# The last two products of a decoder block by seven products for all eight units, and norms summed by two wide matmuls

## The chip, the core and the metric

The kernel runs on one core of a Trainium2 chip. A core has TensorE (PE, matrix products into PSUM), VectorE (DVE), ScalarE (ACT), GpSimd (POOL) and SyncE (SP), which here only issues DMAs; ACT's queue issues the stores. The metric is the time of one execution in microseconds of device time, here the median of three runs.

## The reference

A block over x of 1024 x 2048 in fp32: a norm, one input projection into five parts of width 1024, two branches (a gated MLP and a gated recurrence), a norm of each, an output projection, a norm with residual, and a gated embedding:

```python
hn = rmsnorm(h, pre_g[l])
z = hn @ w_in[l]
u, v, gate_a, xb, gate_b = jnp.split(z, splits, axis=-1)
ya = gmlp_branch(u, v, ...) * jax.nn.silu(gate_a)
yb = rglru_branch(xb, ...) * jax.nn.silu(gate_b)
y = jnp.concatenate([rmsnorm(ya, gmlp_out_g[l]), rmsnorm(yb, lru_out_g[l])], axis=-1)
h = h + rmsnorm(y @ w_out[l], post_g[l])
h = h + (p[l] @ w_pe[l]) * jax.nn.sigmoid(h @ w_pg[l])
```

The change is about the products with `w_out` ("o", weights `w_o1`, `w_o2`) and `w_pg` ("z" or "h", weights `w_g1`, `w_g2`), both 1024 x 2048 by 2048 x 2048, and about the three norms after the first.

## The kernel before, in words

**Precision.** Each fp32 operand is cut in a head and a rest, both of a type that PE takes at one pass (`split`: ACT copies the head, DVE subtracts it from the source, L133 and L124). A product is three: head by head, rest by head, head by rest.

**Quarters and units.** An activation is kept transposed as four quarters q = 2 i + j, where i is the half of the 2048 features and j the half of the 1024 positions; a quarter has four blocks c of 128 x 2 x 512. A unit u is a pair of 128 output columns, one in each half. A unit by the four quarters is a 2x2 product of blocks, eight block products if it is done plainly, seven by the Strassen-Winograd scheme with sums of activations (T1 to T4) and of weights (s1 to s4).

**Steps.** One block product over 1024 features is 24 matmuls of 128x512, and that is a `Step`; a group of n units takes its steps n at a time. `issue` goes through the steps in order: it issues the weight loads three steps ahead, prepares the weights (sums, head and rest) two steps ahead, the activations up to three steps ahead (`lead`), moves spawned tasks on by one (`tick`; a task yields how many steps it waits), and emits the products. `early` holds calls that are to come before a given step; `ahead` fills it. A load by `load_late` waits for the first product of the step before. The framework places the instructions on the engines' queues, which run in order. Buffers: five raw weight tiles, three prepared ones, 32 tiles for activations, four for loads, eight of 512 columns, eight PSUM banks.

**Acts** makes an activation operand when it is first asked for: `fetch` loads the block (scaled by norm and gain the first time, and stored), sums are subtracted on DVE, and `put` splits. For T4, T2 is loaded again from memory.

**The two last products.** In either, units 0 and 1 are plain (`Group.plain`, eight steps with the quarters 21 and 11, and later eight with 22 and 12). Units 2 to 7 go through `set1` (products with 11, 21, T2, T1: 24 steps, with results for two quarters put away) and then `Last2` (with T3, T4, 22: 18 steps). In the last product `OutZ` adds, beside these steps, the products with `w_e` (192 matmuls, L1161), then sigmoid, product and sum with h, and the store.

**Norms.** `norm` sums squares of columns over partitions by narrow products (`rms_small`, L158: a 128x128 block of squares against a column of ones, in fp32), takes the root on 128x4, and spreads the result over partitions with diagonal matrices (`spread`, L173 and L178). `fetch_y` and `fetch_h` then scale with a column of gains and the norm, both on DVE (L1018, L1090).

Of the kernel before, what the change touches and what calls it, by code (L numbers as in the profile page):

```python
# [13 lines left out]
P = 128  # L14
# [3 lines left out]
NH = 8  # L18
# [22 lines left out]
B1 = (2, 2, 2, 1, 1)  # L41
# [7 lines left out]
def block_kernel(ctx: ExitStack, tc: tile.TileContext, xq, pT, w_v, w_l1, w_l2, w_u1, w_u2, w_o1, w_o2, w_g1,  # L49
                 w_g2, w_e, wsT, w_ax, cols, bs, outq):  # L50

# [140 lines left out]
    def norm(accs, n, s, j, wait):  # L192

        yield wait
        small = cpool.tile([P, 4], F32, tag="small", bufs=4, name="small")
# [98 lines left out]
    class Acts:  # L294
# [3 lines left out]
        def __init__(self, name, fetch, t_d=None, made_t=False, wide=None, apart=False):  # L298
            self.fetch, self.made, self.made_t, self.apart = fetch, {}, made_t, apart
            self.wide, self.keep_t1 = wide or t_ld, True  # L300
            self.t1_d, self.t2_d = t_d or [[dram(f"{name}t{n}_{c}", P, 2, TH) for c in range(NC)] for n in (1, 2)]
# [11 lines left out]
        def make(self, v, c):  # L313
            if (v, c) in self.made:
                return
            if v in ("11", "12", "21") or v == "22" and self.apart:
                self.put(v, c, self.fetch({"11": 0, "12": 1, "21": 2, "22": 3}[v], c))
            elif v in ("T1", "T2") and self.made_t:
                self.put(v, c, self.again(self.t2_d if v == "T2" else self.t1_d, c))
            elif v in ("T1", "T2"):  # L320
                x11, x12 = self.fetch(0, c), self.fetch(1, c, self.wide)
                sub(x11, x12, x11)
                x22 = self.fetch(3, c, self.wide)
# [4 lines left out]
                if self.keep_t1:  # L328
                    store.dma_start(out=self.t1_d[c], in_=x11)
                self.put("T1", c, x11)  # L330
            elif v in ("T3", "22"):
# [3 lines left out]
                if not self.apart:  # L335
                    self.put("22", c, x22)
# [5 lines left out]
        def calls(self, v, cs):  # L342
            return [lambda v=v, c=c: self.make(v, c) for c in cs]

    class Group:
# [85 lines left out]
        def plain(self, v1, v2, second, done):  # L431


            tiles, end = range(self.n), self.n - 1
            banks = self.bank(), self.bank()
            first = len(steps)
            for m, (v, k) in enumerate(((v1, second), (v2, 1 - second))):
                for i in range(2):
                    for j in tiles:
                        self.step(banks[i], v, j, (2 * i + k,), heads, m == 0,  # L440
                                  self.each(lambda u, ps, i=i: done(i, u, ps), banks[i], m and j == end))
            return steps[first:]

        def set2(self, p7, p74, p3):

            first = len(steps)
            self.set2_7(p7)
            self.set2_3(p3, True)
            self.set2_4(p74, True)
            return steps[first:]  # L450
# [16 lines left out]
        def set2_4(self, p74, late, hold=False):  # L467

            def prep(a22=None, a12=None):
# [3 lines left out]
                t = self.raws["s4"] = t_act("s4", shape=(P, T)) if hold else a12  # L473
                sub(t, a12, a22, nc.gpsimd)
                if hold:
                    spawn(summed())
                return hl

            def summed():
                yield 1  # L480
                self.s4(self.raws["s4"])
# [3 lines left out]
        def set2_3(self, p3, late, hold=False):  # L485
            pb = self.bank()

            def prep(a12=None, a22=None):
# [5 lines left out]
                return heads(a12 if hold else self.s4(a12))  # L494
# [80 lines left out]
    class Last2:  # L575


        def __init__(self, d, at, n, done):
            self.d, self.at, self.n, self.done, self.t = d, at, n, done, {}

        def load(self):
            for u in range(self.n):
                t = t_act("u42")
                for i, k in enumerate(("u4", "u2")):
                    self.t[u, k] = t[:, i]
                    load_late(t[:, i], self.d[self.at + u][k])

        def p7(self, u, ps):
            t = t_h("c22")
            add(t, self.t[u, "u4"], ps)  # L590
            self.done(self.at + u, 3, t)

        def p74(self, u, ps):
            t = self.t[u, "u2"]
            add(t, t, ps)
            self.done(self.at + u, 2, t)

        def p3(self, u, ps):
            t = self.t[u, "u4"]
            add(t, t, ps)  # L600
            self.done(self.at + u, 1, t)
# [65 lines left out]
    def v_pass(j, n):  # L667
# [28 lines left out]
        for i, c in order:  # L696
# [13 lines left out]
            def post(i=i, c=c):  # L710
                if (i, c) == order[-1]:
                    if n == 0:
                        spawn(norm([accx[j][:, 0], accx[j][:, 1]], D, rb, j, 1))
# [7 lines left out]
    def fetch_x(q, c, new=t_ld):  # L721
        t = new("xn")
# [92 lines left out]
    class Lru:  # L815
# [28 lines left out]
        def rest(self):  # L844
# [24 lines left out]

            nc.scalar.activation(out=th, in_=r, func=AF.Tanh, scale=cs[:, b:b + 1])  # L870
            mul(i, i, xc)
            nc.scalar.activation(out=q, in_=g, func=AF.Sigmoid)
# [58 lines left out]
    class LastU:  # L931
# [20 lines left out]
        def gated(self, n, j):  # L952
# [3 lines left out]
            mul(m, m, u)  # L956
            nc.scalar.activation(out=u, in_=g, func=AF.Sigmoid)
            mul(g, g, u)
# [12 lines left out]
            if h == NH - 1:  # L971
                spawn(norm([acc["a"][:, HALF[j]], *squares_a[j]], D // 2, s_a, j, 2 + j))
# [32 lines left out]

    normed = set()

    def fetch_y(q, c, new=t_ld):
        t = new("y")
# [7 lines left out]
        for e in range(2):  # L1017
            nc.vector.scalar_tensor_tensor(out=t[:, e], in0=t[:, e],  # L1018
                                           scalar=col("lru_out_g" if i else "gmlp_out_g", 2 * c + e),
                                           in1=s, op0=ALU.mult, op1=ALU.mult)  # L1020
# [265 lines left out]
```

## Time and profile before

| | |
|---|---|
| runs | 1609.73, 1611.49, 1617.24 us (median 1611.49) |
| the profiled execution's own time | 1614.6 us |
| its span, first to last instruction | 1612.8 us |
| mean granted clock of PE | 0.985 |
| PE busy | 1553.1 us in 6836 matmuls |
| DVE, ACT, POOL busy | 1125.2, 714.5, 183.6 us |
| HBM read, written | 293.14, 92.80 MB |

The profile is of one execution. Busy shares are means over stages that differ. PE's matmuls overlap, so a wide product shows as 0.39 us while one starts every 0.23 us; times per product are read from runs of products. "Idle before" is time of an engine ahead of an instruction, with what ended it.

### The profile page before, as it was taken

Reading aid. Unit: us, or ns where it says so; the run is one execution under the profiler, and the core shown is the slowest. Engines: PE = TensorE matmul, PEld = TensorE weight load, DVE = VectorE, ACT = ScalarE, POOL = GpSimd, SP = SyncE. Lnnn points to the kernel's source line nnn. Section 1 sums busy time; section 2 is a strip of 40 time slices with the busy share of each in tenths; the row PEclk is TensorE's granted clock in tenths of the full one; section 3 lists DMA queues with packets and bytes.
Section 4 is the critical chain, followed back from the end, with each engine's and each line's share of the span. In section 5 each row is a group of like instructions: output and inputs, shape, how many; then the busy total and the mean of one; then the engine's idle time right before and its main releaser. Section 6 shows DMA issues by size and latency. Waiting matters only on the chain.

```text
span 1612.8 us, 18403 instructions
## 1 busy us (share of the span) xinstructions
PE 1553.1 (96%) x6836; PEld 1271.9 (79%) x6836; DVE 1125.2 (70%) x1226; ACT 714.5 (44%) x861; POOL 183.6 (11%) x93
## 2 busy tenths in 40 slices
PE   7999999999899999999999999999899999999998
PEld 6878877888677777778777888788788788887787
DVE  7897775556778877788488876467547677477664
ACT  5865432224355566657355543254232333453221
POOL 3230000001111212100020012003310000001100
PEclk9999999999899999999999999999998999999999
DMA  7644776678655555458489797588737897798861
GB/s 262 222 169 141 250 249 222 233 232 317 214 177 181 172 175 166 163 208 287 138 280 383 273 344 257 195 322 289 256 128 262 297 357 273 252 368 300 286 239 61
DMA packets 134730, 387.17 MB, mean 240 GB/s; under 512 B 14960, under 2 KB 20208, under 8 KB 134640
## 3 DMA queue, kind: packets, MB, share of 16 engines
q1 hardware_dynamic: 91584, 293.12, 53.6%
q10 hardware_dynamic: 43056, 92.88, 14.9%
q8 instruction: 53, 0.87, 0.2%
q14 instruction: 37, 0.30, 0.1%
HBM read 293.14 MB, written 92.80 MB: 239 GB/s over the span
## 4 chain that ended last, share of the span: by engine, by line
PE 54%; DVE 14%; DMA 13%; issue 9%; POOL 3%; ACT 1%; SPq 0%; DVEq 0%; POOLq 0%; ACTq 0%
PE z L366 44%; PE z L677 5%; DVE w_hl L124 4%; DMA w_raw<-w_l 3%; POOL w_raw L124 2%; DMA w_raw<-w_o 2%; DMA w_raw<-w_u 2%; PE e L1161 2%; DVE w_raw L127 2%; DMA t<-xt 1%; DVE w_raw L124 1%; DVE xc L853 1%; PE g L789 1%; PE g L158 1%; DMA y<-p74m 1%
## 5 line engine op out<-in xcount | busy, mean ns | idle before, releaser
L133 ACT ACTIVATE w_hl<-w_raw 128x1024 fp32r<-128x1024 f32 (+1 forms) x257 | 269.7, 1051 | 332.7 <-PE z L366 170.8
L124 DVE TENSOR_TENSOR w_hl<-w_raw,w_hl 128x1024 fp32r<-128x1024 f32 (+1 forms) x257 | 322.4, 1258 | 100.3 <-ACT w_hl L133 100.0
L366 PE MATMUL z<-a22h,w_hl 128*128 128x512 f32 x576 | 172.3, 389 | 0.0
L366 PE MATMUL z<-a11h,w_hl 128*128 128x512 f32 x576 | 159.4, 391 | 5.0 <-ACT a11h L133 2.7
L366 PE MATMUL z<-a21h,w_hl 128*128 128x512 f32 x576 | 162.9, 397 | 0.9 <-ACT a21h L133 0.9
L127 DVE TENSOR_TENSOR w_raw<-w_raw 128x1024 f32<-128x1024 f32 x52 | 77.8, 1496 | 114.2 <-POOL w_raw L124 71.1
L124 POOL TENSOR_TENSOR w_raw<-w_raw 128x1024 f32<-128x1024 f32 x24 | 64.9, 2703 | 800.5 <-DMA outq<-c 248.7
L366 PE MATMUL z<-aT4h,w_hl 128*128 128x512 f32 x448 | 144.8, 406 | 10.0 <-ACT aT4h L133 5.7
L366 PE MATMUL z<-aT3h,w_hl 128*128 128x512 f32 x448 | 138.9, 391 | 1.2 <-DVE w_hl L124 1.2
L677 PE MATMUL z<-w_hl,xsh 128*128 128x512 f32 x512 | 129.4, 395 | 10.1 <-ACT xsh L662 6.9
L366 PE MATMUL z<-aT2h,w_hl 128*128 128x512 f32 x448 | 126.2, 394 | 5.6 <-DVE w_hl L124 4.8
L366 PEld LDWEIGHTS z<-a11h,w_hl 128*128 128x128 f32 x576 | 107.6, 188 | 29.4 <-ACT a11h L133 4.0
L366 PE MATMUL z<-aT1h,w_hl 128*128 128x512 f32 x448 | 126.9, 392 | 2.5 <-ACT u L133 2.0
L366 PEld LDWEIGHTS z<-a21h,w_hl 128*128 128x128 f32 x576 | 109.7, 191 | 24.1 <-ACT a21h L133 1.3
L366 PEld LDWEIGHTS z<-a22h,w_hl 128*128 128x128 f32 x576 | 108.0, 188 | 22.5
L677 PEld LDWEIGHTS z<-w_hl,xsh 128*128 128x128 f32 x512 | 96.7, 190 | 31.3 <-ACT xsh L662 6.9
L366 PEld LDWEIGHTS z<-aT4h,w_hl 128*128 128x128 f32 x448 | 87.8, 197 | 30.6 <-ACT aT4h L133 7.3
L366 PE MATMUL z<-a22l,w_hl 128*128 128x512 f32 x288 | 107.0, 390 | 0.0
L124 DVE TENSOR_TENSOR w_raw<-w_raw 128x1024 f32<-128x1024 f32 x56 | 68.9, 1230 | 53.7 <-DMA w_raw<-w_l 22.5
L366 PEld LDWEIGHTS z<-aT2h,w_hl 128*128 128x128 f32 x448 | 84.3, 190 | 24.9 <-DVE w_hl L124 6.6
L366 PEld LDWEIGHTS z<-aT1h,w_hl 128*128 128x128 f32 x448 | 83.3, 188 | 21.6 <-ACT u L133 3.7
L366 PEld LDWEIGHTS z<-aT3h,w_hl 128*128 128x128 f32 x448 | 84.4, 188 | 19.7 <-DVE w_hl L124 2.1
(241 smaller groups left out, 2598.0 us busy)
## 6 DMA issues: line engine op xcount, KB each, us to landing
w_raw<-w_l SPq DMA_DIRECT2D x72, 512.0 KB, 4.0
w_raw<-w_u SPq DMA_DIRECT2D x72, 512.0 KB, 4.1
w_raw<-w_o SPq DMA_DIRECT2D x70, 512.0 KB, 4.7
w_raw<-w_g SPq DMA_DIRECT2D x70, 512.0 KB, 5.4
w_raw<-w_v SPq DMA_DIRECT2D x31, 512.0 KB, 3.7
xn<-xn SPq DMA_DIRECT2D x24, 512.0 KB, 5.3
y<-yn SPq DMA_DIRECT2D x24, 512.0 KB, 5.5
h<-h SPq DMA_DIRECT2D x24, 512.0 KB, 5.5
```

Source lines behind the costliest of these rows:

```text
L124: (engine or nc.vector).tensor_tensor(out=out, in0=a, in1=b, op=ALU.subtract)
L127: (engine or nc.vector).tensor_tensor(out=out, in0=a, in1=b, op=ALU.add)
L133: nc.scalar.activation(out=out, in_=src, func=AF.Copy)
L158: nc.tensor.matmul(ps[:, j:j + 1], lhsT=acc[:, j * P:(j + 1) * P], rhs=ones[:, 0:1], start=i == 0, stop=i == len(accs) - 1)
L366: ins = nc.tensor.matmul(ps, lhsT=hl[:, w, o:o + P], rhs=a[x], start=fresh and kp == 0 and n == 0, stop=kp == 7 and n == 2, skip_group_che ...
L677: ins = nc.tensor.matmul(ps, lhsT=a[x][:, e, b * P:(b + 1) * P], rhs=hl[:, w, e * TH:(e + 1) * TH], start=(i, c, e, m) == (0, 0, 0, 0), st ...
L789: nc.tensor.matmul(ps[:, (2 * k + i) * P:(2 * k + i + 1) * P], lhsT=gv[i][:, (h + k) * P:(h + k + 1) * P], rhs=ws[:, h + k], start=True, s ...
L853: nc.vector.scalar_tensor_tensor(out=xc[:, n:], in0=xb[:, :T - n], scalar=cw[j], in1=xc[:, n:], op0=ALU.mult, op1=ALU.add)
L1161: nc.tensor.matmul(ps, lhsT=self.hl[u][:, w, o:o + P], rhs=pa[k][x][:, j], start=k == 0 and n == 0, stop=k == 1 and n == 2)
```

## The change

- In both last products all eight units go through the seven products, in three sets (`Units`, `three_sets`). `set_a`: quarter products with 21 and 11, in groups of two units, 16 steps; their sum is the result of quarter 0, and p1 is put away. `set_b`: T3 and 22, unit by unit, 16 steps; p1 is loaded, p17 and p13 are put away. `set_c`: T2, T4 and T1, 24 steps in an order written out; p17 and p13 are loaded, POOL adds p6 to both, and three results per unit follow. `plain`, `Last2` and its held sums go.
- T2 is made as 11 + T3 (head, then rest) and T4 as 21 - T2 (head, then rest), from tiles that are resident; T1's subtraction goes to POOL. No T is stored or loaded again in these two products.
- `norm` adds the squares, splits the sum, and multiplies head and rest by a matrix of ones: the sum comes out on all partitions at 512 columns, and root and correction are done at that size. The norm of the first stage keeps the old form as `norm_x`.
- Half of the fetches (j = 0) are scaled by POOL (norm) and ACT (gain) instead of DVE. The blocks of x for the residual are loaded seven steps ahead for that half.
- In `Lru` the gate's sigmoid comes ahead of the tanh; in `LastU` a sigmoid becomes a tanh of the half, with the factors folded in the products. The norm of y waits three steps for either half. The last product's outputs (`OutUnits`) come beside the steps with T4 and T1.

```diff
     def norm(accs, n, s, j, wait):
+        yield wait
+        for acc in accs[1:]:
+            add(accs[0], accs[0], acc)
+        hi, lo = (pool.tile([P, TH], F32R, tag="h", bufs=N_H, name="sq" + k) for k in "hl")
+        split(hi, lo, accs[0])
+        yield 1
+        ps, v, r, dst = psum("g"), t_h("var"), t_h("std"), pool.tile([P, TH], F32, tag="s", bufs=4, name="s")
+        for i, a in enumerate((hi, lo)):
+            nc.tensor.matmul(ps, lhsT=ones_r, rhs=a, start=i == 0, stop=i == 1)
+        nc.vector.tensor_scalar(out=v, in0=ps, scalar1=1.0 / n, scalar2=EPS, op0=ALU.mult, op1=ALU.add)
+        nc.scalar.activation(out=r, in_=v, func=AF.Sqrt)
+        nc.vector.reciprocal(out=dst, in_=r)
+        mul(r, dst, dst)
+        mul(r, r, v)
+        nc.vector.tensor_scalar(out=r, in0=r, scalar1=-0.5, scalar2=1.5, op0=ALU.mult, op1=ALU.add)
+        mul(dst, dst, r)
+        s[j] = dst
...
+    class Acts3(Acts):
+        def make(self, v, c):
...
+            if v in ("T1", "T2"):
+                x11, x12, t2 = self.fetch(0, c), self.fetch(1, c), t_ld("t2")
+                t3 = [a.bitcast(F32) for a in self.made["T3", c]]
+                add(t2, x11, t3[0])
+                add(t2, t2, t3[1])
+                self.put("T2", c, t2)
+                sub(x12, x12, x11, nc.gpsimd)
+                self.put("T1", c, x12)
+            elif v == "T4":
+                x21 = self.fetch(2, c)
+                for a in self.made["T2", c]:
+                    sub(x21, x21, a.bitcast(F32))
+                self.put("T4", c, x21)
...
+        def set3_6(self, p6, hold):
+            self.pa = self.bank()
+            def prep(a21, a22, a11):
+                s1 = self.raws["s1"] = t_act("s1", shape=(P, T)) if hold else a21
+                add(s1, a21, a22)
+                sub(a11, s1, a11)
+                self.raws["22"] = a22
+                return heads(a11)
+            self.step(self.pa, "T2", 0, (2, 3, 0), prep, True, self.each(p6, self.pa, True))
+        def set3_4(self, p64):
+            self.step(self.pa, "T4", 0, (), lambda: heads(self.raws.pop("22")), False,
+                      self.each(p64, self.pa, True))
+        def set3_5(self, p5):
+            pb = self.bank()
+            self.step(pb, "T1", 0, (), lambda: heads(self.raws.pop("s1")), True, self.each(p5, pb, True))
...
+    class Units:
...
+            for v, n in ((2, 0), (2, 1), (1, 0), (2, 2), (1, 1), (2, 3), (1, 2), (1, 3)):
...
+        def p1(self, u, ps):
+            p1, t = t_h("p1"), self.t.pop(u)
+            copy(p1, ps)
+            store.dma_start(out=self.d[u]["p1"], in_=p1)
+            add(t, t, ps)
+            self.done(u, 0, t)
+        def set_b(self):
+            for u in range(NH):
+                g = Group(self.w2[u:u + 1], 1, self.acts)
+                n = len(steps)
+                g.set2_7(lambda _, ps, u=u: self.p7(u, ps))
+                g.set2_3(lambda _, ps, u=u: self.p3(u, ps), True)
+                steps[n].acts.append(lambda u=u: self.load1(u))
...
+            order = [(6, 0), (6, 1), (5, 0), (5, 1), (4, 0), (4, 1), (6, 2)]
+            for u in range(2, NH):
+                order += [(6, u + 1)] * (u < NH - 1) + [(4, u)] + [(5, u)] * (u not in self.held)
+            for k, u in order + [(5, u) for u in self.held]:
...
+        def p6(self, u, ps):
+            t = self.t[u, "22"] = t_h("c22")
+            copy(t, ps)
+            add(self.t[u][:, 1], self.t[u][:, 1], t, nc.gpsimd)
+            add(t, t, self.t[u][:, 0], nc.gpsimd)
...
+        def p5(self, u, ps):
+            for q, t in ((3, self.t.pop((u, "22"))), (1, self.t[u][:, 1])):
+                add(t, t, ps)
+                self.done(u, q, t)
...
+    def scale(t, gs, s, spare):
+        if spare:
+            mul(t, t, s.unsqueeze(1).broadcast_to([P, 2, TH]), nc.gpsimd)
+        for e, g in enumerate(gs):
+            if spare:
+                nc.scalar.activation(out=t[:, e], in_=t[:, e], func=AF.Copy, scale=g)
+            else:
+                nc.vector.scalar_tensor_tensor(out=t[:, e], in0=t[:, e], scalar=g, in1=s,
+                                               op0=ALU.mult, op1=ALU.mult)
...
+    def three_sets(units, acts, at):
+        first = len(steps)
+        units.set_a()
+        for n in range(at):
+            steps[first + n].lead = n + 1
+        ahead(range(first - 4 + at, first + at), acts.calls("21", range(NC)))
+        ahead(range(first + at, first + 4), acts.calls("11", range(NC)))
+        ahead(range(first + 6, first + 14, 2), acts.calls("T3", range(NC)))
+        first = len(steps)
+        units.set_b()
+        ahead(range(first + 1, first + 13, 3), acts.calls("T2", range(NC)))
+        first = len(steps)
+        units.set_c()
+        ahead(range(first - 2, first + 2), acts.calls("T4", range(NC)))
+    ay = Acts3("y", fetch_y)
+    three_sets(Units("ou", w_o1, w_o2, ay, done_o, range(4, NH)), ay, 1)
...
+    ahead(range(first - 7, first - 3), [lambda q=q, c=c: load_x2(q, c) for q in (2, 0) for c in range(NC)])
+    three_sets(OutUnits(), ah, 2)
```

## Rows read from the trace of the kernel before

**Rows 1.** The page's first part: busy time, share of the span, instructions.

```profile
PE 1553.1 (96%) x6836; PEld 1271.9 (79%) x6836; DVE 1125.2 (70%) x1226; ACT 714.5 (44%) x861; POOL 183.6 (11%) x93
```

**Rows 2.** The chain that ended last: start us, us, what.

```profile
1202.35 2.12 PE g L158 x20
...
1507.77 5.44 PE z L366 x24
...
1607.08 0.70 DVE u L127
...
1609.19 0.69 DVE u L127
```

**Rows 3.** Line L158's matmuls: duration ns min/median/max, first and last start.

```profile
L158 PE MATMUL g<-ones_r,sq x48: 164/250/353, 1199.3 to 1232.4; 128*128 128x1 f32 x48
...
L158 PE MATMUL g<-ones_r,b x16: 164/250/250, 755.1 to 756.7; 128*128 128x1 f32 x16
```

**Rows 4.** Windows: length, busy us (x) of PE, PEld, DVE, ACT, POOL; PEclk, DMA, GB/s.

```profile
862.00:1607.00 745.00, 728.00 (x3193) 597.37 (x3191) 490.33 (x528) 278.18 (x339) 69.39 (x36) 0.98 0.76 270
...
1113.00:1177.00 64.00, 58.50 (x243) 46.95 (x242) 35.32 (x30) 17.73 (x23) 28.45 (x15) 0.95 0.71 237
...
1224.00:1278.00 54.00, 49.83 (x214) 39.62 (x214) 33.63 (x40) 15.51 (x18) 0.00 (x0) 0.91 0.72 256
1278.00:1437.00 159.00, 158.08 (x697) 130.25 (x696) 106.90 (x102) 66.80 (x78) 0.00 (x0) 1.00 0.87 313
1437.00:1507.00 70.00, 66.70 (x281) 54.13 (x280) 52.77 (x58) 22.13 (x27) 4.80 (x2) 0.95 0.88 314
1507.00:1607.00 100.00, 100.00 (x442) 82.51 (x440) 58.56 (x74) 24.91 (x33) 9.65 (x4) 1.00 0.51 183
```

**Rows 5.** Waits of PE in 862:1613: us in total, times, longest.

```profile
PE z L366 <- DVE c L127: 4.3, 2, 3.6
PE z L366 <- ACT a11h L133: 2.7, 3, 1.3
```

**Rows 6.** Timeline of PE: start us, us, instruction, idle time before it.

```profile
1158.27 0.61 PE L366 MATMUL z<-aT3h,w_hl 128*128 128x512 f32 x2
...
1162.66 1.19 PE L366 MATMUL z<-aT4h,w_hl 128*128 128x512 f32 x2 [3.55 <-DVE c L127]
...
1492.82 1.10 PE L366 MATMUL z<-aT4h,w_hl 128*128 128x512 f32 x2 [2.62 <-ACT aT4h L133]
```

**Rows 7.** Timeline of POOL and DVE about 1143 us.

```profile
1143.11 1.30 POOL L127 TENSOR_TENSOR o<-o,sq 128x512 f32<-128x512 f32 x1
...
1143.19 2.30 DVE L127 TENSOR_TENSOR s<-s,w_raw 128x1024 f32<-128x1024 f32 x1 [5.68 <-POOL s L124]
```

**Rows 8.** Groups by form: count, busy us, mean ns, idle before and its releasers.

```profile
L124 DVE TENSOR_TENSOR w_raw<-w_raw 128x1024 f32<-128x1024 f32 x56 | 68.9, 1230 | 53.7 <-DMA w_raw<-w_l 22.5 <-DMA w_raw<-w_o 17.9 <-DMA w_raw<-w_u 10.7
...
L1018 DVE SCALAR_TENSOR_TENSOR y<-y,cv,s 128x512 f32<-128x512 f32 x32 | 23.9, 779 | 13.4 <-DMA y<-y 12.6 <-ACT s L133 0.8
...
L127 DVE TENSOR_TENSOR u<-u,z 128x512 f32<-128x512 f32 x32 | 21.5, 681 | 22.2 <-PE z L366 22.2
...
L124 POOL TENSOR_TENSOR w_raw<-w_raw 128x1024 f32<-128x1024 f32 x24 | 64.9, 2703 | 800.5 <-DMA outq<-c 248.7 <-DMA xn<-xn 126.7 <-DMA w_raw<-w_u 101.8
L127 POOL TENSOR_TENSOR o<-o,sq 128x512 f32<-128x512 f32 x24 | 38.9, 1622 | 190.5 <-ACT sq L187 190.4
...
L662 ACT ACTIVATE xsh<-xr,cv 128x512 fp32r<-128x512 f32 x64 | 42.4, 710 | 9.5 <-PE z L677 5.7 <-DMA xr<-xq 2.0 <-DVE xn L728 1.7
...
L955 ACT ACT_TABLE_LOAD x7 | 9.0, 1283 | 0.1
```

**Rows 9.** DMA issues by line: KB each, median us to landing.

```profile
w_raw<-w_g SPq DMA_DIRECT2D x70, 512.0 KB, 5.4
```

**Rows 10.** Waits of DVE in 861:1613.

```profile
DVE w_raw L127 <- POOL w_raw L124: 29.5, 6, 7.7
...
DVE h L127 <- DMA x<-xq: 12.0, 5, 3.1
```

More of the change, by code (lines that the diff above doesn't have):

```diff
@@ L493, in prep @@
                     a12 = self.raws.pop("s4")
-                return heads(a12 if hold else self.s4(a12))
+                return heads(self.s4(a12))
             self.step(pb, "22", 0, (1, 3) if late else (), prep, True, self.each(p3, pb, True))
@@ L1016, in fetch_y @@
         s = has(s_b if i else s_a, j)
[L1017 to L1020, printed above, removed]
-        store.dma_start(out=yn_d[q][c], in_=t)
+        scale(t, [col("lru_out_g" if i else "gmlp_out_g", 2 * c + e) for e in range(2)], s, j == 0)
+        if q < 3:
+            store.dma_start(out=yn_d[q][c], in_=t)
         return t
-    o_u = parts("ou", NH, ("u2", "u4"))
     started, squares = set(), {0: [], 1: []}
@@ L1042, in done_o @@
         started.add(j)
-    def plain_o(j):
-        def done(i, u, ps):
-            t = t_h("o")
-            copy(t, ps)
-            done_o(u, 2 * i + j, t)
-        return done
-    ay1 = Acts("y", fetch_y, wide=t_act)
-    first = len(steps)
-    ahead(range(first - 4, first), ay1.calls("21", range(NC)))
-    Group(w_o1[0:2], 2, ay1).plain("21", "11", 1, plain_o(0))
-    ahead(range(first, first + 4), ay1.calls("11", range(NC)))
-    ahead(range(first + 5, first + 17, 3), ay1.calls("T2", range(NC)))
@@ L1057, in block_kernel @@
-    set1(w_o1, 2, B1[1:], ay1, lambda at, n: First1(o_u, at, lambda u, t: done_o(u, 0, t)), 4)
-    ay2 = Acts("y", fetch_y, (ay1.t1_d, ay1.t2_d), apart=True)
-    first = len(steps)
-    ahead(range(first - 3, first - 1), ay2.calls("22", range(NC)))
-    ahead(range(first - 1, first + 1), ay2.calls("12", range(NC)))
-    Group(w_o1[0:2], 2, ay2).plain("22", "12", 1, plain_o(1))
-    ahead(range(first + 1, first + 8), ay2.calls("T3", range(NC)) + ay2.calls("T4", range(NC)))
-    two = [(Group(w_o2[at:at + 1], 1, ay2), Last2(o_u, at, 1, done_o)) for at in range(2, NH)]
@@ L1095, in fetch_h @@
         return t
-    z_u = parts("zu", NH, ("c11", "c21", "u2", "u4"))
-    def put_z(u, k, t):
-        store.dma_start(out=z_u[u][k], in_=t)
-    def plain_z(i, u, ps):
-        t = t_h("z")
-        copy(t, ps)
-        put_z(u, ("c11", "c21")[i], t)
-    ah1 = Acts("h", fetch_h, wide=t_act)
-    ah1.keep_t1 = False
-    first = len(steps)
-    ahead(range(first - 2, first + 4), ah1.calls("21", range(NC)) + ah1.calls("11", range(NC)))
-    Group(w_g1[0:2], 2, ah1).plain("21", "11", 1, plain_z)
-    steps[first].lead = 2
-    ahead(range(first + 4, first + 16, 3), ah1.calls("T2", range(NC)))
-    set1(w_g1, 2, B1[1:], ah1, lambda at, n: First1(z_u, at, lambda u, t: put_z(u, "c11", t)), 4)
-    ah2 = Acts("h", fetch_h, (ah1.t1_d, ah1.t2_d), apart=True)
+    ah = Acts3("h", fetch_h)
     pa = []
@@ L1158, in product_e, with beside @@
+        def beside(self, u, j):
+            for i in range(2):
+                ps = self.e[u, 2 * i + j] = psum("e")
                 for k in range(2):
```

252 lines of the change are left out of this document (111 added, 141 removed).

## The prediction

> **What bounds the kernel now.** I read the page's engine line first: TensorE (PE) is busy 96% of the span, DVE 70%, ACT 44%, POOL 11% [rows 1]. The reader is to see a kernel that waits for one engine, and so two questions: how many PE instructions does the change take out, and does PE still get its operands in time afterwards?
>
> For the first I went to the chain of work that ended last. In its undisturbed parts one step, 24 products of 128x512, takes 5.44 us, so one wide product costs 0.2267 us; twenty of the narrow products of L158 take 2.12 us, 0.106 us each [rows 2].
>
> For the second I took the window from the steps that lead into the product with w_out (I call this the entry; the passage is the way from it to the last product) to the last step, 862 to 1607 us: 745.0 us with 3193 matmuls, of which 112 narrow ones (the 128 of L158 that are not accx's, less sixteen at 755 us [rows 3, 4]). 3081 x 0.2267 + 112 x 0.106 = 710.3 us is the work; **34.7 us is loss**: PE idle, or at the lower of its two clock levels. By the same count 8.9 us of it lies in 1113:1177 (64.0 - 243 x 0.2267), 10.3 us in 1224:1278 (54.0 - 174 x 0.2267 - 40 x 0.106), 6.3 us in 1437:1507, and 1.0 us in the whole of 1278:1437 [rows 4]. So the loss sits in three places, and there the waits name the cause: a DVE addition that reads the bank late, and activations of the next product that come late [rows 5]. The timeline shows what such a wait does besides: after 3.55 us of idle time two products take 1.19 us where they took 0.61 before [rows 6], and the granted clock of that stretch is 0.95, of the 1224 one 0.91 [rows 4]: a part at 1.2 GHz instead of 2.4.
>
> **What the change takes from PE.**
> 1. Steps. Each of the last two products has 58 steps: plain units 0 and 1 take 8+8, six units take 24+18. After it has 16+16+24 = 56. Four steps go: 4 x 5.44 = **-21.8 us**. This work is on PE at the top clock, and nothing else moves into its place; the products with w_e stay as many.
> 2. Norms. The three norms outside the first stage, each in two halves, sum through narrow products: 48 + 5 x 16 = 128 of them [rows 3], 128 x 0.106 = 13.6 us. Twelve wide products on diagonals are replaced by twelve wide ones on head and rest, equal in number and shape. **-13.6 us.** The bound below: those near 870 and 1228 stand just ahead of waits, so PE may only wait sooner; the 24 and 40 there are worth 6.8 us. Between 6.8 and 13.6 I take the upper end: what PE waits for behind them is itself made late by the same norms, so the waits move forward with them.
> 3. End. The last step closes one tile now (addition 1607.08, last addition 1609.19 [rows 2]). After, the last step closes two, q=3 and q=1; DVE has six pieces of 0.70 us instead of three with a sigmoid between: **+1.4 us**.
>
> Sum: -34.0 us.
>
> **What it adds elsewhere, and what hides it.** Per last product:
> - DVE, added: four sums of weights for each of two more units, 8 x 1.23 = 9.8; one more operation per block for the T's, 4 x 1.23 = 4.9; 24 more additions from PSUM at 0.68 = 16.3; two norms that work on 512 columns instead of 4, some ten operations of 0.68 each less the diagonals, +10. Removed: two rests of weights 2.5, four rests of activations 4.9 (1.23 each), and 16 half-block scalings at 0.78 = 12.5 that go to POOL and ACT [rows 8]. Net +21 us, so 490 becomes about 532 us of a window of 711: 75%. PE hides it on average. A reciprocal of 512 columns has no row; below it is another 0.68, above I allow 5 us, on two norms that something waits for.
> - POOL: eight scalings, four T1 subtractions and two more weight subtractions at 2.70 (the scalings by the nearest row, a subtraction of that size), 16 additions at 1.62: 64 us, where the window has 69 for both products [rows 4, 8]. ACT: 16 scaled copies at 0.71, 11 us [rows 8]; at 278 of 745 us [rows 4] it hides them. But its queue is in order: a scaled copy that waits for POOL holds up the heads of weights behind it, which PE wants two steps (10.9 us) later; POOL's 2.7 us doesn't reach that far.
> - DMA: four reloads fewer of each of four blocks, two more weight tiles, and spills p1, p17, p13. The second set asks for four weight tiles per 10.9 us, each 5.4 us to land [rows 9]; with prepared weights two steps ahead I cost it at nothing, and a chain on it below. The earlier loads of x pass weight tiles on SP's queue: eight issues, a few us in all, inside the same two steps.
> - The blocks x2 are loaded seven steps early for half of the blocks. Now DVE waits 12.0 us for them [rows 10]. What is late next there is the longer way through POOL: 2.7 + 1.4 + 1.23 + 2.3 us a block, blocks following each other at POOL's 2.7, which is what PE takes for half a step. So I keep the loss of this passage.
> - The gates (an order of activations in Lru, a tanh for a sigmoid in LastU): as many instructions on DVE and ACT as before. At most the seven table loads of L955 and as many of L957, 1.28 us each [rows 8], go from ACT, which doesn't bound that stage: nothing, or some 2 us of waits at the entry, within the range.
> - DVE in the second set: a unit (10.9 us of PE) asks for two rests 2.5, two sums 2.5, two PSUM additions 1.4, and T2/T1 4.9 per three steps, 3.3: 9.6 us. In the first set of the last product the T3 blocks need 9.3 us each (four half scalings, two additions of x, one subtraction, two rests): four with eleven rests of weights and a few additions make 55 us in the 58 us from step 6 until the last block is needed in step 16. It fits in both places, barely.
>
> What DVE does while POOL works is shown once: POOL's addition ran from 1143.11 for 1.30 us, and a DVE addition with both inputs in SBUF, started at 1143.19, took 2.30 us instead of 1.23 [rows 7, 8]. By the Trainium skill, page "SBUF — State Buffer", section "Who interferes with whom", such a DVE operation and a reading POOL operation exclude each other for the whole instruction; the trace agrees, with 1.07 us lost to 1.30. If all 128 us of new POOL work met DVE so, DVE would stand at 660 of 711 us, 93%, and the likeliest sum would still hold on average.
>
> **Why the losses stay.** Of the three places, the wait for the DVE addition (1162) goes with its step order; the set with T3 and the chain behind POOL come in its stead. The passage to the last product keeps its norm and its eight fresh blocks. The T4 wait (1492) goes, T4 now reading resident heads; instead the second set runs the form with POOL's subtraction in the chain sixteen times. So I take 34.7 us again: bounds 10 us (the passage alone keeps its 10.3) and, if DVE is late, 34.7 + 29.
>
> **Rivals.**
> - *DVE and POOL get in each other's way in the second set.* Per unit POOL does 1.67 operations of 2.7 us there. If all block DVE, a unit needs 9.6 + 4.5 = 14.1 us, 3.2 too many; 8 x 3.2 less the two steps prepared ahead (10.9) is +14.7 us a product, 29 for both; if half do, nothing. I put +6 to +26: 1583 to 1603. For it: the 29.5 us that DVE already waits for POOL's sums in six places [rows 10]. Against: additions from PSUM have one SBUF input, and DVE waits for that sum anyway.
> - *The old losses go and few new ones come.* Resident T's spare 16 loads a product, x comes early: loss 10 to 20 instead of 34.7, 1553 to 1563. Against: every tight place above.
> - *Nothing measurable.* Both products lose some 26 to 42 us more, 1603.5 to 1619.5: the full 29, with some low clock behind it.
> - *Slower.* The late sum becomes a stop in every unit: a landing 5.4, POOL 2.7, DVE's addition 2.3 and the two halves of the head 2.3 make 12.7 us against 10.9. At that, 1.8 x 16 = 29, less what is ahead. But where the form ran with a third step and T4 between, PE stood 2.62 us for one block [rows 6]; at 3.3 us for each of sixteen units (the 2.62 and a part of the low clock behind it, at most 0.05 x 70 = 3.5 us [rows 4]) it is +53, 1630. It decides from 34.0 / 16 = 2.1 us a unit. Against it: the units at 1507 to 1607 run in the same form, with a third step, without loss (442 x 0.2267 = 100.2 of 100.0 us [rows 4]).
>
> **How the numbers follow.** The profiled execution took 1614.6 us (span 1612.8); less 34.0 it is 1580.6. The median of the three runs, 1611.5, lies 3.1 lower, so I predict **1577.5 us**. Chances: losses as now 0.50 (its own range 1568 to 1588, by the 6.8 us of item 2 and by 10 us of loss more or less), losses gone 0.15, DVE and POOL 0.20, nothing 0.08, slower 0.07. This kernel's runs tell 0.5%, 8 us, from no change: faster 0.85, same 0.08, slower 0.07. The range 1556 to 1603 leaves out the last two and the edge of the second.
>
> **What would show it.** Four steps fewer (96 wide products of L366 under a new number) and no narrow ones after the first stage; the window from the end of the stage before to the last step about 711 us. Right: loss of some 35 us, at the entry, the passage and the ends of the first sets. Wrong: PE waiting for rests of w_hl throughout the second sets, DVE there over 90% busy, w_raw sums of 2.3 us by the dozen; or a clock under 0.9 in one of the sets, which would say that stops repeat in every unit.

## The result and the profile after

The changed kernel takes 1658.06 us (median of 4 runs, 1654.26 to 1658.69) where the kernel before took 1613.75 beside it: a ratio of 1.0271 (95% interval 1.0239 to 1.0302). It is 44 us slower, where I predicted 34 us faster. Times of the kernel before differ between the groups of runs (medians 1614 to 1620), so each kernel below is told by its ratio too.

The page's engine line of the kernel after, which answers to [rows 1]:

```profile
PE 1535.3 (93%) x6612; PEld 1245.7 (75%) x6612; DVE 1237.5 (75%) x1252; ACT 710.7 (43%) x866; POOL 326.7 (20%) x153
```

PE has 224 instructions fewer: 96 of four steps and 128 narrow ones, as foretold. DVE has 112 us more and POOL 143. The window from the same place (the steps ahead of the product with w_out) to the last step, which answers to the first of [rows 4], with the same columns, and then its stretches, cut at the first product of each set (the four steps ahead, then first, second and third set of o, and of z):

```profile
862.70:1649.10 786.40, 710.45 (x2985) 571.64 (x2983) 590.78 (x555) 280.36 (x352) 207.40 (x96) 0.96 0.69 240
...
862.70:885.00 22.30, 22.30 (x100) 18.41 (x99) 16.87 (x19) 11.54 (x16) 9.54 (x4) 1.00 0.91 343
885.00:993.00 108.00, 93.47 (x388) 74.80 (x386) 94.14 (x94) 59.80 (x79) 23.91 (x10) 0.94 0.69 235
993.00:1105.40 112.40, 93.89 (x385) 74.19 (x384) 83.86 (x68) 28.83 (x31) 36.94 (x15) 0.94 0.74 254
1105.40:1251.50 146.10, 132.90 (x580) 107.91 (x578) 99.47 (x85) 51.11 (x65) 64.28 (x37) 0.98 0.64 216
1251.50:1359.80 108.30, 95.34 (x387) 75.25 (x387) 91.77 (x85) 47.01 (x61) 16.45 (x6) 0.93 0.80 288
1359.80:1463.80 104.00, 94.35 (x385) 75.09 (x385) 85.36 (x69) 27.96 (x29) 30.11 (x11) 0.95 0.78 279
1463.80:1649.10 185.30, 178.20 (x769) 146.00 (x767) 119.31 (x140) 54.11 (x73) 26.17 (x16) 0.98 0.57 193
```

The work is 2985 x 0.2267 = 676.7 us, near the 710.3 - 21.8 - 13.6 = 674.9 of the prediction. The window is 41 us longer all the same: **the loss is 109.7 us (786.4 - 676.7) instead of 34.7**. It begins 0.7 us later than before, so no cost of the changed gates and of the first of the three norms is seen ahead of it. By set (a set has 386, 384, 578, 386, 384 and 768 products that start in it; the rows count up to two more that reach over an edge) it is 20.5, 25.4 and 15.0 us in o, 20.8, 17.0 and 11.2 in z. The clock of the first two sets of each product is 0.93 to 0.95, so a part of the loss is PE at the lower of its two levels (1.2 of 2.4 GHz) behind a stop, as at 1162 before [rows 6].

What PE waited for from 862 us to the end, the three longest sums (total, times, longest):

```profile
PE z L407 <- DVE w_hl L125: 38.6, 24, 3.4
PE z L407 <- ACT a21h L134: 16.1, 2, 8.6
PE z L407 <- ACT w_hl L134: 16.0, 8, 4.4
```

Before, the longest of such sums between 862 and 1613 was 4.3 us [rows 5]. All of these waits come to 76.0 us of the 109.7. Now the heads and rests of the weights come late, and the first blocks of the next product. Two places show how.

**A unit of the second set.** Timelines of POOL, DVE, ACT and PE about 1010 us (in brackets the idle time ahead and what ended it):

```profile
1009.69 2.38 POOL L125 TENSOR_TENSOR w_raw<-w_raw 128x1024 f32<-128x1024 f32 x1 [10.28 <-DMA w_raw<-w_o]
...
1012.11 2.28 DVE L128 TENSOR_TENSOR w_raw<-w_raw 128x1024 f32<-128x1024 f32 x1 [7.23 <-POOL w_raw L125]
...
1014.91 2.77 DVE L128 TENSOR_TENSOR t<-y,aT3h 128x1024 f32<-128x1024 f32 x1
...
1019.81 1.21 DVE L125 TENSOR_TENSOR w_hl<-w_raw,w_hl 128x1024 fp32r<-128x1024 f32 x1
...
1015.39 0.63 ACT L188 ACTIVATE sq<-c 128x512 f32<-128x512 f32 x1 [10.12 <-DVE c L128]
1015.93 1.04 ACT L134 ACTIVATE w_hl<-w_raw 128x1024 fp32r<-128x1024 f32 x1
...
1021.08 0.79 PE L407 MATMUL z<-a22h,w_hl 128*128 128x512 f32 x1 [3.36 <-DVE w_hl L125]
```

POOL starts at 1009.7, as the tile of a22 has landed, and subtracts; DVE has stood 7.23 us for that and adds in 2.28 instead of 1.23, while POOL's next addition (1012.04, 1.27 us) runs beside it; then its queue runs two additions from PSUM and two of a T2 block, the head waits on ACT behind the square of one of them, and the rest comes at 1019.81. From the landing to PE's product it is 11.4 us, longer than a unit of PE (10.9). And the landing was late because the chain holds the buffers: the load was issued at 1003.18, when a subtraction of the unit before (DVE, 1001.93, 1.23 us) had given a tile back. What the loads on SP's queue waited for in that set:

```profile
SPq L306 <- DVE w_hl L125: 44.9, 16, 7.3
SPq L306 <- POOL w_raw L125: 19.1, 7, 3.5
```

A unit takes four raw tiles, and there are five; a load waits for a tile that the chain of the unit before gives back. Not every unit is late: PE waits for a head or a rest in five of this set's eight. Landings are not slower than before in the median (4.4 us after 4.7 for w_o; for w_g the line below answers to [rows 9]), though this one took 6.4 us; issues by line, KB each, median us to landing:

```profile
w_raw<-w_g SPq DMA_DIRECT2D x72, 512.0 KB, 4.5
```

**The passage.** Timelines of DVE, POOL, and ACT at the end of o:

```profile
1229.80 3.35 DVE L207 RECIPROCAL s<-std 128x512 f32<-128x512 f32 x1 [0.76 <-ACT std L206]
...
1240.88 3.03 DVE L125 TENSOR_TENSOR w_hl<-w_raw,w_hl 128x1024 fp32r<-128x1024 f32 x1
1243.84 2.83 DVE L128 TENSOR_TENSOR o<-o,sq 128x512 f32<-128x512 f32 x1
1246.60 3.36 DVE L128 TENSOR_TENSOR h<-h,x 128x1024 f32<-128x1024 f32 x1
...
1240.44 11.72 POOL L131 TENSOR_TENSOR h<-h,s 128x1024 f32<-128x1024 f32 x4 [1.56 <-DVE s L131]
...
1250.36 1.06 ACT L134 ACTIVATE a21h<-h 128x1024 fp32r<-128x1024 f32 x1 [2.87 <-DVE h L128]
```

The norm's sum is on PE at 1226, the scale is there at 1240; four multiplications on POOL take 2.93 us each, and the rest and the additions that DVE runs beside them take 2.8 to 3.4 where 0.68 (o) and 1.23 (the others) is their time alone. The first head of a21 is made 24 us after the norm's sum; PE waits 8.6 us, and the two steps there, the last of o with this wait and the first of z, take 14.24 and 10.66 us instead of 5.44.

### The profile page after: what moved, and what is told of

Read it like the earlier page. It is cut to its first block, busy times and chain, and to the rows that moved or that the text cites. A ratio compares the mean times of both kernels' runs of the same rounds, so it can differ in the third digit from the quotient of the medians.

```text
span 1656.2 us, 18147 instructions
## 1 busy us (share of the span) xinstructions
PE 1535.3 (93%) x6612; PEld 1245.7 (75%) x6612; DVE 1237.5 (75%) x1252; ACT 710.7 (43%) x866; POOL 326.7 (20%) x153
## 4 chain that ended last, share of the span: by engine, by line
DVE 25%; DMA 18%; PE 17%; issue 8%; ACT 3%; POOL 3%; SPq 0%; ACTq 0%; DVEq 0%; POOLq 0%
PE z L407 14%; DVE w_hl L125 7%; DMA w_raw<-w_o 4%; POOL w_raw L125 3%; DMA w_raw<-w_g 2%; PE e L1243 2%; DVE w_raw L128 2%; DMA w_raw<-w_l 2%; DMA w_raw<-w_u 2%; DVE w_raw L125 2%; DMA h<-h 1%; DVE p L128 1%; DVE t L128 1%; DMA yn<-y 1%; DVE xc L951 1%
## 5 line engine op out<-in xcount | busy, mean ns | idle before, releaser
L125 DVE TENSOR_TENSOR w_hl<-w_raw,w_hl 128x1024 fp32r<-128x1024 f32 (+1 forms) x253 | 341.9, 1353 | 57.2 <-ACT w_hl L134 56.9
L125 POOL TENSOR_TENSOR w_raw<-w_raw 128x1024 f32<-128x1024 f32 x32 | 87.1, 2723 | 512.1 <-DMA xn<-xn 127.9
L128 DVE TENSOR_TENSOR w_raw<-w_raw 128x1024 f32<-128x1024 f32 x60 | 90.0, 1501 | 110.0 <-POOL w_raw L125 72.3
L407 PE MATMUL z<-aT2h,w_hl 128*128 128x512 f32 x512 | 154.6, 399 | 17.7 <-DVE w_hl L125 10.1
L407 PE MATMUL z<-aT3h,w_hl 128*128 128x512 f32 x512 | 161.3, 394 | 8.4 <-DVE w_hl L125 5.4
L407 PE MATMUL z<-aT4h,w_hl 128*128 128x512 f32 x512 | 160.5, 395 | 3.8 <-ACT aT4h L134 3.1
L407 PE MATMUL z<-a21h,w_hl 128*128 128x512 f32 x512 | 144.7, 402 | 20.2 <-ACT a21h L134 17.2
L407 PE MATMUL z<-a11h,w_hl 128*128 128x512 f32 x512 | 143.1, 397 | 9.6 <-DVE w_hl L125 7.9
L407 PE MATMUL z<-aT1h,w_hl 128*128 128x512 f32 x512 | 150.0, 390 | 1.5 <-DVE w_hl L125 1.5
L407 PEld LDWEIGHTS z<-aT1h,w_hl 128*128 128x128 f32 x512 | 95.8, 188 | 22.5 <-DVE w_hl L125 2.4
L125 DVE TENSOR_TENSOR w_raw<-w_raw 128x1024 f32<-128x1024 f32 x60 | 74.1, 1235 | 50.5 <-DMA w_raw<-w_l 23.0
L407 PE MATMUL z<-aT4l,w_hl 128*128 128x512 f32 x256 | 101.2, 395 | 3.8 <-DVE aT4l L125 3.8
```

What stands on the lines that cost most here:

```text
L125: (engine or nc.vector).tensor_tensor(out=out, in0=a, in1=b, op=ALU.subtract)
L128: (engine or nc.vector).tensor_tensor(out=out, in0=a, in1=b, op=ALU.add)
L407: ins = nc.tensor.matmul(ps, lhsT=hl[:, w, o:o + P], rhs=a[x], start=fresh and kp == 0 and n == 0, stop=kp == 7 and n == 2, skip_group_che ...
```

## Experiments

The theories: **A**, POOL's scaling holds DVE and the new blocks up at the entry and the passage; **B**, POOL's subtraction stands in a chain that the five raw tiles make longer than a unit; **C**, the wide norm with its reciprocal takes back what the narrow products gave; **D**, DVE simply has too much to do. Loss by set, in us, is the length from a set's first product to that of the next, less 0.2267 a product (0.106 a narrow one), each from one profiled execution; "ahead" are the last three or four steps ahead of o. A profiled execution can lie anywhere among its kernel's runs: that of 2 (1632.7 us) is the slowest of ten, that of 9 (1630.0) the fastest of four.

| kernel | median us | ratio to before (95%) | ahead | o 1 | o 2 | o 3 | z 1 | z 2 | z 3 |
|---|---|---|---|---|---|---|---|---|---|
| the change | 1658.1 | 1.0271 (1.0239–1.0302) | 0.1 | 20.5 | 25.4 | 15.0 | 20.8 | 17.0 | 11.2 |
| 1 scaling on DVE | 1643.8 | 1.0156 (1.0104–1.0208) | 1.8 | 9.1 | 23.5 | 8.8 | 15.9 | 22.5 | 13.9 |
| 2 second sets without POOL | 1626.0 | 1.0040 (1.0013–1.0067) | 0.1 | 21.5 | 8.7 | 13.9 | 21.9 | 4.4 | 11.0 |
| 3 narrow norms | 1662.1 | 1.0270 (1.0219–1.0321) | 10.5 | 8.4 | 22.1 | 9.1 | 27.6 | 17.0 | 10.8 |
| 4 all three | 1620.9 | 1.0009 (0.9983–1.0034) | 8.4 | 9.7 | 5.5 | 10.0 | 21.3 | 4.4 | 10.1 |
| 5 = 1 + 2 | 1613.9 | 0.9960 (0.9936–0.9984) | 5.8 | 6.8 | 11.0 | 8.3 | 14.2 | 9.2 | 10.9 |
| 6 = 2 + idle POOL work | 1632.6 | 1.0082 (1.0058–1.0105) | 0.1 | 20.8 | 14.2 | 14.3 | 21.3 | 9.7 | 7.1 |
| 7 before + wide norm | 1625.2 | 1.0030 (1.0008–1.0051) | | | | | | | |
| 8 = 5, T1 forward | 1612.3 | 0.9971 (0.9945–0.9996) | 2.0 | 8.0 | 9.6 | 10.1 | 17.0 | 8.3 | 9.4 |
| 9 = 2, weights alone | 1637.2 | 1.0119 (1.0082–1.0156) | 0.6 | 21.5 | 9.9 | 13.2 | 21.7 | 6.5 | 10.6 |
| 10 = 5, T3 swap | 1610.6 | 0.9941 (0.9914–0.9968) | 5.3 | 7.7 | 8.2 | 11.7 | 18.1 | 5.4 | 10.9 |
| 11 = 10, T2 steps apart | 1603.0 | 0.9904 (0.9872–0.9935) | 5.9 | 6.9 | 3.9 | 9.8 | 18.5 | 6.1 | 9.4 |
| 12 = 11, T3 spread | 1600.7 | 0.9868 (0.9841–0.9894) | 5.6 | 7.2 | 8.3 | 6.7 | 16.7 | 5.1 | 6.1 |

**1. Scaling on DVE.**

```diff
-        scale(t, [col("lru_out_g" if i else "gmlp_out_g", 2 * c + e) for e in range(2)], s, j == 0)
+        scale(t, [col("lru_out_g" if i else "gmlp_out_g", 2 * c + e) for e in range(2)], s, False)
...
-        scale(t, [col("post_g", 8 * i + 2 * c + e) for e in range(2)], has(s_o, j), j == 0)
+        scale(t, [col("post_g", 8 * i + 2 * c + e) for e in range(2)], has(s_o, j), False)
```

> All blocks of y and h are scaled on DVE (16 half-block scalings of 0.78 a product instead of 8 POOL multiplications and 16 scaled copies on ACT). Theory A (POOL's four multiplications of 2.9 us in a row hold DVE off at the entry, 885:938, and at the passage, 1237:1296): the loss of these two places, 13.5 and 19.7 us over their products, falls by half or more, PE's 8.6 us wait for the head of a21 goes, total 12 to 25 us less, 1633 to 1646. Theory C (the wide norm's reciprocal is what the chain waits for): up to 6 us less, 1652 to 1660, and the first block of a21 still comes late. Theory D (DVE has simply too much to do): the 25 us more of DVE work make it 5 to 20 us slower, 1663 to 1678.

By the profiled executions 14.5 us of loss go: 11.4 in the first set of o, 6.2 and 4.9 about the passage, with 5.5 more in the second set of z. PE's wait for the head of a21 at the passage is now 3.3 us instead of 8.6:

```profile
PE z L407 <- ACT a21h L134: 3.3, 1, 3.3
```

A holds, D falls: some 25 us more of scalings on DVE, and less time. Whether it is POOL's own 2.9 us in each block's chain or the DVE instructions held beside it is not told apart here; the rows of the passage show both.

**2. Second sets without POOL.**

```diff
-                    sub(a12, a12, a22, nc.gpsimd)
+                    sub(a12, a12, a22, None if self.dve else nc.gpsimd)
...
                 g = Group(self.w2[u:u + 1], 1, self.acts)
+                g.dve = True
...
-                sub(x12, x12, x11, nc.gpsimd)
+                sub(x12, x12, x11)
```

> In the second set of both products no subtraction is on POOL: the sixteen of weights and the eight of T1 blocks go to DVE (24 x 1.23 = 30 us more on DVE, 24 x 2.6 us less on POOL). Theory B (POOL's 2.4 to 3.3 us in the weight chain, through five raw buffers, is what the second sets lose 25 + 17 us to): their loss falls to under 15 together, total 25 to 40 us less, 1618 to 1633. Theory A in the second set (DVE's operations double while POOL works): the same sign, w_hl rests there at 1.2 instead of 1.4 us on average. Theory D (DVE is full there, 83.5 of 112 us busy): 87 us of PE work want 98 us of DVE, the loss stays within 5 us of 42 or grows, 1655 to 1675. The entry and the passage keep their loss.

Their losses fall from 42.4 to 13.1 us, and nothing else moves by more than 1.1 us. Windows of the two sets in this kernel:

```profile
997.20:1092.90 95.70, 90.55 (x385) 72.66 (x384) 82.34 (x78) 26.90 (x28) 3.93 (x3) 0.98 0.83 293
1347.30:1438.80 91.50, 89.84 (x385) 73.00 (x386) 81.59 (x80) 28.11 (x29) 0.00 (x0) 0.98 0.89 310
```

DVE does ten and eleven instructions more in them and is busy for less time (82.3 against 83.9 us, 81.6 against 85.4), at 86 and 89% of the window. D falls here too. The loads of the first of these sets still wait 59 us for raw tiles, where it was 72; no run changed the number of these tiles, so what more of them would give is not known.

**6. The same, with POOL work that nobody waits for.**

```diff
...
+                hl = heads(self.s4(a12))
+                if self.dve:
+                    for i in range(4):
+                        w = hl[:, 1, 256 * i:256 * (i + 1)].bitcast(F32)
+                        add(dead, w, w, nc.gpsimd)
+                return hl
```

> The second sets without POOL in the chain, as in the run before with that edit alone, but after each late head POOL does four additions of 256 columns on the rest just made, whose results nobody uses: some 2.5 to 3 us of POOL a unit, as much as the subtraction that was taken off it, and beside DVE's work instead of ahead of it. Theory B (the subtraction cost by its place in the chain): the second sets lose at most 8 us more than without it, 1624 to 1635. Theory A (POOL and DVE exclude each other, and that is what cost): 20 to 30 us come back, 1645 to 1656, and DVE's additions there take 1.6 us and more on average.

It was meant to tell B from mere exclusion. The POOL group in the second set of z, and the window of that set:

```profile
L130 POOL TENSOR_TENSOR dead<-w_hl 128x256 f32<-128x256 f32 x32 | 40.4, 1264 | 138.8 <-DVE w_hl L127 137.0
```

```profile
1346.20:1443.00 96.80, 92.53 (x385) 74.28 (x386) 88.94 (x80) 28.12 (x29) 40.44 (x32) 0.96 0.85 297
```

By its records this is more POOL time than the change's in that set (40.4 against 30.1 us), and it costs 5.5 + 5.3 = 10.8 us of loss in the two sets, not 29.3, and 6.6 us by the medians. The time is in the range of B (1624 to 1635), the loss over its 8 us. DVE's time there grows by 7.4 us. The Trainium skill, "SBUF — State Buffer", section "Who interferes with whom", has a DVE operation with two SBUF inputs and a reading POOL operation shut each other out; the trace agrees: one such DVE addition at 1393.01 took 1.63 us beside a POOL group, where 1.21 is its time alone.

But this POOL work shuts DVE out less than the change's did. The rests of the weights in the second set of z, in the change, in 6 and in 2:

```profile
L125 DVE TENSOR_TENSOR w_hl<-w_raw,w_hl 128x1024 fp32r<-128x1024 f32 x17 | 29.6, 1746 | 0.0
```

```profile
L127 DVE TENSOR_TENSOR w_hl<-w_raw,w_hl 128x1024 fp32r<-128x1024 f32 x17 | 21.7, 1292 | 2.9 <-ACT w_hl L136 2.8
```

```profile
L125 DVE TENSOR_TENSOR w_hl<-w_raw,w_hl 128x1024 fp32r<-128x1024 f32 x17 | 20.5, 1220 | 2.4 <-ACT w_hl L134 2.2
```

And a POOL record holds the time in which POOL itself is kept waiting: the same addition of 256 columns took 0.61 us in 21 of the 64 cases. Adding up over both second sets what each DVE operation took beyond its 1.22 us (1024 columns) or 0.68 (512), I get 30 us in the change, 15 in 6 and 2 in 2. So run 6 tests exclusion at half its size, and by itself it does not say whether the place in the chain or exclusion is the larger part of the 29.3 us. It does show that POOL work costs time even where nobody waits for its results.

**9. Only the weight subtraction moved.** The edit of 2 without its T1 lines.

> The changed kernel with only the sixteen weight subtractions of the second sets on DVE; the eight subtractions of T1 blocks stay on POOL. Theory B (the place in the weight chain costs): nearly all of the 29.6 us that the two edits together gave back in the second sets comes from this one, 1626 to 1633, their losses at most 12 and 7. If DVE's being held off by POOL's T1 subtractions is what costs: half of it or less, 1640 to 1656.

The losses of the second sets are 9.9 and 6.5 us: 26.0 of the 29.3 us come from the sixteen weight subtractions. This bears on the question that 6 left: DVE's operations are still lengthened by 19 us there, and these 17 us more than in 2 cost 3.3 us of loss; the 11 us more in the change come with 26.0. That speaks for the place in the chain, without proving it, since a longer operation can cost more at one place than at another. The median is 11 us above that of 2 all the same, and over the 1626 to 1633 expected; the profiled execution, with a span of 1628.0, lies at the runs' lower end (1630.0 to 1641.2), that of 2 at their upper end, so what T1 is worth, 3 us by the losses or up to 11 by the times, stays open.

**3, 4 and 7. The norm.** In 3 and 4 the three calls take the old norm (`norm_x`) again (s_o is shown; s_b alike, s_a with its old waits too); in 7 the kernel before takes the new one. The edit of 3 and 4:

```diff
-    spawn(norm([acc["o"][:, HALF[j]], *squares[j]], D, s_o, j, 1))
+    spawn(norm_x([acc["o"][:, HALF[j]], *squares[j]], D, s_o, j, 1))
```

> The three norms outside the first stage sum through narrow products again, as in the kernel before: 128 products of 0.106 us more on PE, 13.6 us, and six reciprocals of 512 columns of 3.35 us less on DVE. Theory C (the wide norm lies on the chain at the entry and the passage): the waits there shrink by more than the 6.8 us that the narrow products near them cost, total 5 to 15 us less, 1643 to 1653. Rival (the wide norm is worth what was predicted, and the loss is elsewhere): 7 to 14 us slower, 1665 to 1672.

> The three edits together: scaling on DVE, no POOL in the second sets, narrow norms. Theory A with B and C: the changes add, 40 to 70 us less, 1588 to 1618, at or under the kernel before. Theory D: at most 15 us less, DVE over 80% busy in the second sets and PE still waiting there for rests of w_hl.

> The kernel before with the wide norm alone, no other part of the change: 128 products of 0.106 us go from PE, six reciprocals of 512 columns come to DVE. The prediction's item 2: 7 to 14 us less, ratio 0.991 to 0.996. Theory C (the reciprocal in the chain takes back what the products gave): ratio 0.998 to 1.003.

Alone on the kernel before, the wide norm takes 128 products from PE and the time goes up by 0.3% (0.1 to 0.5). The largest item that comes in for them, in the kernel with the wide norm alone:

```profile
L206 DVE RECIPROCAL s<-std 128x512 f32<-128x512 f32 x6 | 20.0, 3344 | 0.8 <-ACT std L205 0.8
```

Put back into the changed kernel, the narrow norm leaves the ratio where it was (1.0270 after 1.0271): its products cost PE 12 us more, the losses are 4 us less, at other places, and the window of that execution begins 5 us earlier. Neither range on record for 3 was met (1643 to 1653, or 1665 to 1672; it was 1662). In company of the other two edits the narrow norm costs 7 us (4 against 5), and 4 ends 3 us above its 1588 to 1618. So C has its expected ratio in 7 (0.998 to 1.003), and in the first two pairs the -13.6 us of the prediction's item 2 are not had. In the third, half of them are. That it is the reciprocal that takes them back is argued from its length; no run changed it alone.

**5. The two edits that help, together.** Edits 1 and 2.

> Scaling on DVE and the second sets without POOL, with the wide norm kept. If the two edits act in different places (the one at the entry and the passage, the other in the second sets), their gains of about 15 and 30 us add: 1658 - 45 = 1613, ratio to the kernel before 0.995 to 1.003; losses by set of about 9, 9, 9 and 16, 5, 12. Theory D (DVE then has some 45 us more per kernel and its queue becomes the wait): 1625 to 1640, with the second product's first set losing over 25.

The gains add: 14 + 32 us expected of the two medians, 44 measured. The kernel is now about as fast as the one before, a little faster. Its window:

```profile
860.20:1602.90 742.70, 701.28 (x2985) 568.82 (x2983) 580.01 (x611) 262.66 (x320) 89.03 (x56) 0.97 0.73 255
```

Beside the change's 590.78 us (x555): DVE runs 56 instructions more in less time, since POOL's 118 us less no longer lengthen them.

**8, 10, 11 and 12. What is left.** On top of 5:

```diff
 # 8
-order = [(6, 0), (6, 1), (5, 0), (5, 1), (4, 0), (4, 1), (6, 2)]
+order = [(6, 0), (5, 0), (6, 1), (5, 1), (4, 0), (4, 1), (6, 2)]
 # 10, in Acts3.make
+            elif v in ("T3", "22"):
+                x12, x22 = self.fetch(1, c), self.fetch(3, c)
+                self.put("22", c, x22)
+                sub(x12, x22, x12)
+                self.put("T3", c, x12)
 # 11, with 10
+order = [(6, 0), (5, 0), (6, 1), (4, 0), (5, 1), (6, 2), (4, 1)]
 # 12, with 10 and 11
-ahead(range(first + 6, first + 14, 2), acts.calls("T3", range(NC)))
+ahead(range(first + 5, first + 16, 3), acts.calls("T3", range(NC)))
```

> As the first kernel of this group, and in the third sets the product with T1 of unit 0 comes ahead of unit 1's with T2, so that the three weight tiles that each T2 step needs are asked for in alternate steps instead of six in a row. If the six tiles through five buffers are what delays the first two steps of the third sets (8.2 and 8.0 us instead of 5.4, twice), 5 to 12 us less than without it; if DVE's blocks of T4 are, within 3 us.

> Scaling on DVE and second sets without POOL; in a T3 block the head and rest of x22 are made before the subtraction that overwrites x12, which waits for x12's store to have been read (three waits of 3.3 us on DVE in the first set of the last product). If those stops of DVE's queue are what delays the last T3 block at the end of the first set and the start of the second (some 13 us of loss there), 4 to 10 us less than without it, 1603 to 1610, ratio 0.989 to 0.994. If DVE's sum of work is what delays it, within 3 us.

> As the kernel with the T3 swap, and in the third sets no two steps with T2 stand next to each other (6 0, 5 0, 6 1, 4 0, 5 1, 6 2, 4 1, then as before), so that the pair (6 2, 6 3), which took 11.0 and 8.5 us in the last product with unit 0's T1 moved forward, is apart. If two such steps in a row ask for more weight tiles (six, and two of w_e) than five buffers bring in time: 5 to 12 us less than the swap alone. If not: within 3 us.

> As the best kernel so far (scaling on DVE, second sets without POOL, T3 swap, T2 steps apart), and the four T3 blocks of each first set are asked for at steps 5, 8, 11 and 14 instead of 6, 8, 10 and 12: 16.3 us for each instead of 10.9. If the last product's first set ends late because DVE has four blocks of 9.3 us in 55 us (its steps there take 9.0, 8.4 and 10.0 us instead of 5.4), 4 to 10 us less, 1593 to 1599. If the stops for DMA in the block's own chain delay it, the last block comes only later: no change or up to 8 us more.

8 and 10 miss: each within 4 us of 5, their intervals over its own. In 10 the stop that the edit was to remove did not go; DVE's waits between 1230 and 1330 us, in kernel 10 and then in 5:

```profile
DVE h L125 <- DMA h<-h: 9.3, 4, 3.0
```

```profile
DVE h L125 <- DMA h<-h: 7.9, 3, 3.2
```

So the edit did not test what it was for. 11 and 12 are each a step of some 6 us by their ratios (8 and 2 by the medians) that their intervals do not separate from the one before; 12 ends at 1600.7, just over its 1593 to 1599; from 5 to 12 together the ratio falls from 0.9960 to 0.9868, beyond both intervals, and the losses from 66 to 56 us. Neither part can be named alone as the cause. Kernel 12 beats both kernels: 1.3% (1.1 to 1.6) faster than before. Its window:

```profile
860.90:1593.00 732.10, 697.15 (x2985) 566.96 (x2983) 581.15 (x611) 264.38 (x320) 93.38 (x56) 0.98 0.75 259
```

The loss is 732.1 - 676.7 = 55.4 us, 17 of it in the first set of z with the passage, where PE still waits for the chain of the norm and the first blocks (8.9 us between 1190 and 1322) and for a rest of the weights (3.7 us).

## Why the prediction was wrong

- **What goes from PE** was right: 96 + 128 products, work within 2 us of the sum, and at the end 6.9 us from the last product to the span's end against 5.8, +1.1 where I had +1.4.
- **The step that failed is "So I take 34.7 us again"**, the paragraph on why the losses stay: they are 109.7 us. Two of its supports fell one by one, and they are not all of it: with both POOL edits (kernel 5) the loss is still 742.7 - 676.7 = 66.0 us, and what makes it 31 more than I kept is only found in part (kernel 12: 55.4).
- *"With prepared weights two steps ahead I cost it at nothing"*: POOL, addition, head and rest took 11.4 us from the landing in the unit shown, and 17.9 from the issue of the load, where the rival "slower" had put 12.7: POOL and the addition were near what it had, the landing took 1.0 longer, and head and rest took 6.7 us instead of 2.3, as other work stood ahead of them on ACT and DVE. The load itself had waited for a buffer that the chain holds. The two second sets lost 42.4 us, 2.65 a unit, past the 2.1 from which that rival decides. It had the mechanism, though the stops come in some units and not in every one, and I gave it 0.07. What I held against it, units in the same form without loss at 1507 to 1607 [rows 4], had a third step each: 16.3 us for a chain that here has 10.9.
- *"blocks following each other at POOL's 2.7"* and *"So I keep the loss of this passage"*: POOL's multiplications took 2.85 us (h) and 3.34 (y) on average and DVE's operations beside them more than twice their time. The two first sets lost 41 us; scaling on DVE alone takes 16 of these away. "POOL's 2.7 us doesn't reach that far" failed in another form: at 1015.39 a head stood on ACT behind a square that waited for DVE, which waited for POOL.
- **Narrow norms, -13.6 us**: the products went and the time did not, in two of three pairs. I had bounded the reciprocal (another 0.68 to 5; it is 3.35) but not laid the ten operations end to end at the places where the next product waits for them.
- **DVE "+21 us" a product, "PE hides it on average"**: the 532 us became 591, and 75% of a longer window. The sum of busy time was not the limit (kernels 5 and 12 give DVE 56 instructions more); what stood ahead in its queue was. The sentence that the likeliest sum "would still hold" at 93% was no argument.
- **The rival of DVE and POOL in the second set** had the right place and too small a price (+6 to +26), and whether its cause, exclusion, is the lesser part is not settled: run 6 has it cost 10.8 us at half its size, run 9 speaks for the place in the chain. Of the signs of being wrong, PE did wait for heads and rests in the second sets (31 us), but DVE was 75 and 82% busy there, not over 90, only two of the sixteen sums behind POOL took 2.3 us, and no set's clock fell under 0.9.

## What to carry over

An engine's free time on average does not hide work that stands in a chain: write the chain of one unit end to end, from the landing of its tile to the product, with what is queued ahead of each link on its engine, and compare it with the time of one unit in that very form and with the buffers that it holds. Give the slower engine (here 2.39 us for what takes DVE 1.22) only what nobody waits for, and count what it costs the other even then (run 6). Instructions taken from the bounding engine count only where it doesn't wait just behind them.

## What was not expected of the hardware

- A reciprocal of 128x512 on DVE takes 3.35 us, five times the 0.68 of a multiplication of that shape.
- POOL's multiplication of 128x1024 with a broadcast operand took 2.85 us on average for h and 3.34 for y, where its subtraction of that size took 2.78. These averages hold time in which DVE kept POOL waiting: the shortest are 2.39, 2.42 and 2.36 us, so the operand does not make it slower.
- A POOL addition of 256 columns took 0.61 us in 21 of 64 cases, a quarter of 2.39, but 1.47 in the middle: beside DVE's work the record of either engine shows the time it was kept out as busy time.
